# One layer of a hybrid streaming encoder: three MLP banks, one ring of four for scores and transposes, and a block's row factors in one bank

## The chip, the cores and the metric

The kernel is one program on one core of a Trainium2 chip. The metric is the device time of one execution in microseconds (us). Its time before is the median of three runs. One more execution was recorded by the hardware profiler, and all rows shown here are from that execution.

The names of the engines are those of the profile: PE is TensorE's matrix multiplication and PEld its loading of weights, DVE is VectorE, ACT is ScalarE, POOL is GpSimd, SP is SyncE, whose queue (SPq) starts nearly all DMA transfers of this kernel.

## What is computed

One layer of an encoder over a prompt of 2048 tokens and a sample of 32, at a width of 1024. Cut to what matters:

```python
a = rmsnorm(h, g_attn)                 # per token: h * r * g, r = rsqrt(mean(h*h) + eps)
qa, ka, va, qb, kb, vb = split(a @ w_in)
# group A, long range: 4 heads, two q/k maps of 64 dims per head, 128-dim values
s = einsum('bqhmd,bkhmd->bhmqk', qa, ka) * 64 ** -0.5 + t5_bias
p = softmax(where(key_chunk <= query_chunk, s, NEG))
oa = (p[:, :, 0] - lam * p[:, :, 1]) @ va
# group B, band: 8 heads of 64, a chunk of 64 sees itself and the 8 chunks before it
ob = softmax(qb @ kb.T * 64 ** -0.5 + clip_bias) @ vb
h = h + concat(rmsnorm(oa) * (1 - lam_init), rmsnorm(ob)) @ w_out
h = h + square(relu(rmsnorm(h, g_mlp) @ w_up)) @ w_down          # width 4096
h = h + sigmoid(h @ w_ple_gate) * (p_emb @ w_ple_proj)
y = rmsnorm(h, g_final)
```

The keys and values of the prompt and the sample are outputs too; the sample also attends to 128 cached positions. All is float32.

## The kernel before

**Numbers.** A float32 product is made of three matmuls on rounded halves: each operand is split into a high part and the rest (`split`), and `mm3` (lines 212 to 218) accumulates high x high, high x rest and rest x high into one PSUM tile. So a weight piece of 512 KB is loaded by SP (`wr`), its high part (`wh` or `piece`) is written by ACT at line 181, and the rest (`wl`) by POOL or DVE.

**Blocks.** The tokens are cut into four blocks of 512; the last has the 32 sample tokens too. Activations stand transposed, features on partitions.

**Stages.** `prep` loads a block's tokens in tiles of 128, transposes them (`xp`), splits them (`aH`, `aL`) and makes each token's factor r: ACT squares and sums the row, `rsqrt` makes r in ACT and DVE steps (`rsv`, `rsy`), and it lands in a column of `rcol`, one token a partition. To scale products whose tokens lie along a row, the column is spread and transposed into a PSUM tile `rp` (line 393), and ACT copies it to the block's row tile `rbt` (line 394). `proj` makes q, k and v; its evictions of q and k (`qps`, lines 477 and 482) multiply by that row. `attn_a` is the long-range part: JA0 does the query pairs 0 to 3 (256 queries each), JA1 the pairs 4 and 5 and then 6, 7 and the sample (index 8), each for four heads. `attn_b` is the band part. `outproj`, `mlp` (`ups` is an up product, `dps` a down product), `gate` (`gps`, `pps`) and `final` (`yp`) follow by block.

**A pair in the long-range part** (`attn_a_pair`, lines 597 to 729). For each of two query tiles and two maps: score matmuls into a PSUM tile `s` of 512 keys (line 639), eviction by DVE into `e` with the running maximum (lines 646 and 648), exponential on ACT (654), the two maps joined on DVE (660). Then for each four key tiles: transposes of `e` into a PSUM tile `tpp` (698), its halves `pH` by ACT (705) and `pL` by DVE (706), and the products with v into `o` (712 to 714). A sum of squares (`ss`) and a normalisation end the pair. The keys of a head come in tiles of 1024 (`ka`, three buffers), the queries in `q` (two buffers).

**PSUM.** All pools together have eight banks, tiles of 128 x 512 float32. `mm` has two, and a third, `mmx`, joins it in a ring until the second half of the band part is done; then it is given to the long-range scores as `psy`. Scores have `ps_s` (two), transposes `ps_t` (two), outputs `ps_o` (one). A tile of a ring waits until its bank's last user has been read. When attention is over, six banks are opened again as `md`.

**Order.** The program is written as one sequence, but a scheduler with a model of the engines' times orders each engine's instructions before the run. So the output projections and MLPs of blocks 0 and 1, which need nothing of JA1, are spread by it among the scores of JA1 on PE. On the chip each engine and the SP queue go strictly in that order: an instruction that waits holds up all behind it.

## Time and profile before

| | |
|---|---|
| median of three runs | 3122.03 us (3116.57 to 3123.8) |
| the profiled execution | 3116.1 us |
| its span, first to last instruction | 3114.0 us |
| instructions | 51781 |
| long-range scores of JA1 on PE | 1229.88 to 1888.3 us |
| last output matmul of JA1 on PE | 1928.8 us |
| gate of block 1 on PE | from 2029.2 us |

How to read the rows that follow: a row of stages or windows has its stretch in us, its width, and the busy time of PE, PEld, DVE, ACT and POOL with their counts, then the granted clock of TensorE (1 is full), the busy share of the DMA engines and GB/s. A row of waits has the waiting engine, tile and line, what ended the wait, then total us, times, and the longest. A row of the timeline has start, duration, engine, line, operation, output and inputs, and in brackets the idle time of that engine just before, with what ended it. A row of a tile has shortest, median and longest duration in ns, and first and last start.

### The profile page before, as it was taken

To read this page: it belongs to the slowest core of one execution; us is meant where nothing else is said; L and a number is where in the kernel's file an instruction comes from. 1 tells how busy PE (TensorE), PEld (TensorE's weight loads), DVE (VectorE), ACT (ScalarE), POOL (GpSimd) and SP (SyncE) were. 2 spreads that over 40 slices of the span, in tenths; PEclk is the share of its full clock that TensorE was granted. 3 is DMA by queue.
4 is the path that set the end of the run, shared out by engine and by line. 5 is a ranking of instruction groups with operands and counts; after the bars stand their busy time and mean duration, and the time that the engine had idled before them with its cause. 6 is when DMAs were issued, how large, how long until landed. Compare 5 with 4: busy or idle time off the path is not lost. (4 is left out here: it accounts for less than half of the span.)

```text
span 3114.0 us, 51781 instructions
## 1 busy us (share of the span) xinstructions
PE 2992.9 (96%) x17801; PEld 2639.7 (85%) x17801; DVE 1815.1 (58%) x4404; ACT 1779.4 (57%) x3446; POOL 1859.1 (60%) x2512
## 2 busy tenths in 40 slices
PE   8998988999999999999999999999899999999998
PEld 7787877999877887788788888779788887999998
DVE  5256574654466554566655654425667884576663
ACT  6256665765666774566655645454655545554545
POOL 2456745423445543665645556677878888767674
PEclk9999999999999999999999999999999999999999
DMA  9797866976788555565665443538434446333231
GB/s 285 261 263 226 243 199 211 269 225 197 213 248 268 154 148 139 151 172 147 192 173 146 126 122 108 162 98 261 154 116 136 139 159 223 117 109 102 89 117 57
DMA packets 523278, 539.19 MB, mean 173 GB/s; under 512 B 38748, under 2 KB 401568, under 8 KB 523016
## 3 DMA queue, kind: packets, MB, share of 16 engines
q1 hardware_dynamic: 523016, 535.89, 57.3%
q8 instruction: 141, 2.31, 0.3%
q14 instruction: 121, 0.99, 0.1%
HBM read 421.97 MB, written 117.75 MB: 173 GB/s over the span
## 5 line engine op out<-in xcount | busy, mean ns | idle before, releaser
L176 POOL TENSOR_TENSOR wl<-wr,wh 128x256 fp32r<-128x256 f32 x648 | 482.3, 776 | 322.6 <-ACT wh L181 271.2
L181 ACT ACTIVATE piece<-wr 128x512 fp32r<-128x512 f32 x406 | 245.8, 625 | 269.2 <-PE ups L217 116.0
L176 POOL TENSOR_TENSOR piece<-wr,piece 128x256 fp32r<-128x256 f32 x404 | 326.5, 834 | 101.9 <-ACT piece L181 80.7
L181 ACT ACTIVATE wh<-wr 128x1024 fp32r<-128x1024 f32 x228 | 240.5, 1056 | 224.7 <-PE ups L217 56.8
L166 POOL TENSOR_TENSOR wl<-wr,wh 128x256 fp32r<-128x256 f32 x264 | 197.2, 777 | 166.9 <-ACT wh L181 162.0
L216 PE MATMUL dps<-uh,piece 128*128 128x272 f32 (+1 forms) x768 | 246.4, 324 | 7.2 <-ACT piece L181 2.9
L166 POOL TENSOR_TENSOR piece<-wr,piece 128x256 fp32r<-128x256 f32 x280 | 234.4, 868 | 27.8 <-ACT piece L181 24.9
L1158 DVE TENSOR_TENSOR h<-h,dps 128x512 f32<-128x512 f32 x256 | 174.2, 683 | 130.1 <-PE dps L218 128.6
L218 PE MATMUL dps<-uh,piece 128*128 128x272 f32 (+1 forms) x768 | 247.1, 324 | 1.3 <-POOL piece L166 1.1
L217 PE MATMUL dps<-ul,piece 128*128 128x272 f32 (+1 forms) x768 | 247.3, 323 | 0.2 <-DVE ul L187 0.2
L216 PE MATMUL ups<-cs,piece 128*128 128x256 f32 (+1 forms) x864 | 245.7, 285 | 1.6 <-DVE r L1217 1.6
L217 PE MATMUL ups<-cs,piece 128*128 128x256 f32 (+1 forms) x864 | 245.7, 285 | 0.0
L218 PE MATMUL ups<-cs,piece 128*128 128x256 f32 (+1 forms) x864 | 245.5, 284 | 0.0
L216 PE MATMUL qps<-aH,wh 128*128 128x512 f32 (+1 forms) x640 | 228.6, 357 | 1.2 <-DVE ql L477 0.9
L217 PE MATMUL qps<-aL,wh 128*128 128x512 f32 (+1 forms) x640 | 227.2, 355 | 0.0
L218 PE MATMUL qps<-aH,wl 128*128 128x512 f32 (+1 forms) x640 | 227.0, 355 | 0.0
L1206 DVE TENSOR_TENSOR h<-h,dps 128x272 f32<-128x272 f32 (+1 forms) x384 | 189.1, 514 | 51.9 <-PE dps L218 51.1
L216 PE MATMUL dps<-uh,wh 128*128 128x512 f32 x512 | 211.6, 413 | 7.0 <-ACT relu L1123 4.4
L654 ACT ACTIVATE e<-e,nm 128x128 f32<-128x128 f32 (+16 forms) x136 | 157.1, 1156 | 97.4 <-DVE nm L652 96.9
L217 PE MATMUL dps<-ul,wh 128*128 128x512 f32 x512 | 203.5, 397 | 0.0
L218 PE MATMUL dps<-uh,wl 128*128 128x512 f32 x512 | 203.1, 397 | 0.0
L216 PE MATMUL ups<-cH,wh 128*128 128x512 f32 x512 | 202.0, 395 | 0.5 <-ACT relu L1123 0.5
(310 smaller groups left out, 9370.5 us busy)
## 6 DMA issues: line engine op xcount, KB each, us to landing
wr<-w_up SPq DMA_DIRECT2D x128, 512.0 KB, 3.9
wr<-w_down SPq DMA_DIRECT2D x128, 512.0 KB, 3.8
wr<-w_in SPq DMA_DIRECT2D x74, 512.0 KB, 5.5
q<-qS SPq DMA_DIRECT2D x128, 256.0 KB, 5.6
v<-vSa SPq DMA_DIRECT2D x64, 512.0 KB, 3.6
ka<-kS SPq DMA_DIRECT2D x32, 512.0 KB, 8.0
wr<-w_out SPq DMA_DIRECT2D x32, 512.0 KB, 5.0
wr<-w_ple_gate SPq DMA_DIRECT2D x32, 512.0 KB, 4.2
```

The source lines that it names most:

```text
L166: nc.gpsimd.tensor_tensor(out[:, sl], a[:, sl], b[:, sl], op=op)
L176: nc.gpsimd.tensor_tensor(out[:, sl], a[:, sl], b[:, sl], op=op)
L181: nc.scalar.activation(hi, raw, AF.Copy)
L216: nc.tensor.matmul(ps, lh, rh, start=start and i == 0, stop=False)
L217: nc.tensor.matmul(ps, lh, rl, start=False, stop=False)
L218: nc.tensor.matmul(ps, ll, rh, start=False, stop=stop and i == n - 1)
L654: nc.scalar.activation(row, row, AF.Exp, bias=nmx, accum_out=z[:nr, m : m + 1])
L1158: nc.vector.tensor_tensor(hv, hv, ps, op=ALU.add)
L1206: nc.vector.tensor_tensor(hv, hv, ps, op=ALU.add)
```

## The change

There are two edits.

In `prep` the transposes of the row factors are kept in a list while the block's tiles are made. After the fourth tile one PSUM tile `rp` is taken, the four transposes write its four quarters, and one copy of 512 columns goes to `rbt`. Block 3 takes another tile for the sample's 32 tokens.

In `run` the ring of `mm` and `mmx` keeps its three banks through the output projections, norms and MLPs of blocks 0 and 1, and the gate of block 1. The long-range part JA1 takes scores and transposes alike from one ring of four, `ps_s`, `ps_t`, `ps_s`, `ps_t` in turn. The gate of block 1 stands ahead of the closing of the attention pools, in the ring of three, where it had the six banks of `md`.

```diff
@@ prep
         aH, aL = acts[b]
+        late = []
         for i, (c0, n) in enumerate(toks(b)):
...
             self.rsqrt(pp, st[:n], 1, 1.0 / D, EPS, nc.vector, "r1", n, out=r)
+
+            def spread(r=r, c0=c0, n=n):
+                nc.tensor.transpose(rp[:, c0 % 512 : c0 % 512 + n], r.broadcast_to([n, P]), self.ident[:n, :n])
+
+            late.append(spread)
+            yield
+        rp = mm.tile([P, 512], F32, tag=tag, name="rp")
+        for f in late[:4]:
+            f()
+        nc.scalar.activation(self.rb[b][:, :512], rp, AF.Copy)
+        if b == 3:
             rp = mm.tile([P, 512], F32, tag=tag, name="rp")
-            nc.tensor.transpose(rp[:, :n], r.broadcast_to([n, P]), self.ident[:n, :n])
-            nc.scalar.activation(self.rb[b][:, c0 : c0 + n], rp[:, :n], AF.Copy)
-            yield
+            late[4]()
+            nc.scalar.activation(self.rb[b][:, 512 : 512 + SS], rp[:, :SS], AF.Copy)
@@ run
-            mz = mm
+            mm0 = mz = mm
             mm = Rings((mz, "mm"), (mz, "mm"), (opened(mmx, "mmx", 1, PSUM), "mm"))
...
-            mmx.close()
-            mm = mz
-            ps_y = opened(psx, "psy", 1, PSUM, "right")
-            sy = Rings((ps_s, "s"), (ps_s, "s"), (ps_y, "s"))
+            mz = mm
+            sy = Rings((ps_s, "s"), (ps_t, "tp"), (ps_s, "s"), (ps_t, "tp"))
...
-                    self.attn_a(js, pool, sy, ps_t, ps_o)
+                    self.attn_a(js, pool, sy, sy, ps_o)
...
+            drain(self.gate(1, h, uq, actq, mm))
             psx.close()
+            mmx.close()
+            mm = mm0
             md = opened(top, "md", 8 - MM, PSUM, "right")
-            drain(self.gate(1, h, uq, actq, md))
             drain(self.final(1, h, uq, fk, mm))
```

Since the scheduler orders all anew, instructions move far beyond these lines. Three places follow, the second on two engines, each before and then changed; the line numbers in the changed rows are up to 2 higher inside `prep` and 11 higher between it and `run`. (On PE from the middle of `final(1)` on, about 2140 us, the two orders are the same.)

PE at the second token tile of block 2, where a row factor is transposed (`rp`), among products for v and the long-range part JA0. Before:

```order
L713 MATMUL o_2532<-pL_2536,v_2533 128x128
L714 MATMUL o_2532<-pH_2535,v_2533 128x128
L379 MATMUL xp_4656<-ident_113,x_4637 128x128 x4
L393 MATMUL rp_4680<-ident_113,rcol_124 128x128
L698 MATMUL tpp_2778<-ident_113,e_2683 128x128
L216 MATMUL vps_4701<-wh_4685,aH_107 128x256
L217 MATMUL vps_4701<-wl_4686,aH_107 128x256
L218 MATMUL vps_4701<-wh_4685,aL_108 128x256
```

Changed, the place where block 2's four factors are transposed, among the matmuls of its first q product:

```order
L217 MATMUL qps_5032<-aL_108,wh_5022 128x512
L218 MATMUL qps_5032<-aH_107,wl_5023 128x512
L216 MATMUL qps_5032<-aH_107,wh_5022 128x512
L395 MATMUL rp_5105<-ident_113,rcol_124 128x128 x4
L650 MATMUL s_2974<-ka_2952,q_2955 128x384 x2
L650 MATMUL s_2978<-ka_2952,q_2955 128x256 x2
L217 MATMUL qps_5032<-aL_108,wh_5022 128x512
L218 MATMUL qps_5032<-aH_107,wl_5023 128x512
```

The transpose stood directly behind the tile's own token transposes and ahead of an attention transpose; now four stand together, after the fourth tile, between a q product and scores.

The SP queue where the last head of the long-range part starts: `ka_16305` and `ka_16277` are its second key tile, `q_16313` and `q_16285` the queries of its pair 6, `q_16544` those of pair 7. Before:

```order
L157 DMA v_16121<-vSa_86 128x4x256
L157 DMA wr_21799<-w_up 128x8x128
L157 DMA ka_16305<-kS_85 64x2x1024 x2
L157 DMA q_16313<-qS_84 64x2x512
L157 DMA ks_16306<-kS_85 64x2x160 x2
L157 DMA q_16313<-qS_84 64x2x512
L157 DMA q_16544<-qS_84 64x2x512 x2
L157 DMA wr_21841<-w_down 128x2x512
```

Changed:

```order
L157 DMA wr_22518<-w_down 128x2x512
L157 DMA wr_22559<-w_up 128x8x128
L157 DMA ka_16277<-kS_85 64x2x1024 x2
L157 DMA q_16285<-qS_84 64x2x512 x2
L157 DMA wr_22601<-w_up 128x8x128
L157 DMA wr_22643<-w_down 128x2x512
L157 DMA v_16123<-vSa_86 128x4x256
L157 DMA oT_88<-os_15942 128x256
```

The sample's keys (`ks`) and the next pair's queries, which stood between and right behind these queries, now come later, and weights stand there.

PE at the same head's start, from the last score on the head before (`ka_15752`, `ka_15724`) to the first on its own keys (`ka_16304`, `ka_16276`). Before, with 20 further rows of down products left out:

```order
L639 MATMUL s_16078<-ka_15752,q_15991 128x512 x2
L639 MATMUL s_16243<-ks_15753,q_16232 32x160 x2
L639 MATMUL s_16249<-ks_15753,q_16232 32x160 x2
L216 MATMUL dps_21692<-uh_21434,wh_21677 128x512
L217 MATMUL dps_21692<-ul_21435,wh_21677 128x512
L218 MATMUL dps_21692<-uh_21434,wl_21678 128x512
...
L639 MATMUL s_16322<-ka_16304,q_16313 128x512 x2
L639 MATMUL s_16330<-ka_16305,q_16313 128x384 x2
```

Changed, with up and down products, transposes and outputs left out:

```order
L650 MATMUL s_16050<-ka_15724,q_15963 128x512 x2
L216 MATMUL ups_22446<-cH_20378,wh_22437 128x512
L217 MATMUL ups_22446<-cL_20379,wh_22437 128x512
L218 MATMUL ups_22446<-cH_20378,wl_22438 128x512
...
L650 MATMUL s_16215<-ks_15725,q_16204 32x160 x2
...
L725 MATMUL o_16062<-pH_16126,v_16123 128x256
L650 MATMUL s_16221<-ks_15725,q_16204 32x160 x2
L650 MATMUL s_16294<-ka_16276,q_16285 128x512 x2
L216 MATMUL ups_22570<-cH_20378,wh_22561 128x512
```

From 28 matmuls the distance went to 143.

ACT in the gate of block 1, where `sig` is the sigmoid's tile, `wh` a weight piece, and `ou` the split attention rows of block 2 (from `oraw`, loaded for it). Before:

```order
L181 ACTIVATE wh_23415<-wr_23413 128x1024
L1351 ACTIVATE sig_23347<-gps_23322 128x512
L1352 ACTIVATE sig_23347<-sig_23347 128x512
L1353 ACTIVATE sig_23347<-sig_23347 128x512
L1356 ACTIVATE sig_23347<-sig_23347 128x512
L181 ACTIVATE wh_23424<-wr_23422 128x1024
L1351 ACTIVATE sig_23397<-gps_23372 128x512
L181 ACTIVATE wh_23474<-wr_23472 128x1024
```

Changed:

```order
L1362 ACTIVATE sig_23312<-gps_23287 128x512
L1363 ACTIVATE sig_23312<-sig_23312 128x512
L1364 ACTIVATE sig_23312<-sig_23312 128x512
L181 ACTIVATE ou_20426<-oraw_20442 128x512
L181 ACTIVATE ou_20427<-oraw_20446 128x512
L1367 ACTIVATE sig_23312<-sig_23312 128x512
L181 ACTIVATE ou_20428<-oraw_20450 128x512
L181 ACTIVATE ou_20429<-oraw_20454 128x512
L181 ACTIVATE wh_23389<-wr_23387 128x1024
```

The splits of block 2's attention rows stood among the MLP of block 1 before, and now stand inside the chain from a gate product to its sigmoid.

## The prediction

> **What bounds the kernel now.** I read the page's first part, then the span by stages, then what TensorE (PE) waited for, then its timeline at the longest waits.

> ```profile
> PE 2992.9 (96%) x17801; PEld 2639.7 (85%) x17801; DVE 1815.1 (58%) x4404; ACT 1779.4 (57%) x3446; POOL 1859.1 (60%) x2512
> core 0: 3114.0 us, clock 0.986
> ```

> TensorE is busy 96% of the span and no other engine passes 60%. So 3114.0 - 2992.9 = 121.1 us of TensorE idleness, and the stretches in which its granted clock is below 1, are all that a new order can win; the work itself is 17801 matmuls in both kernels. From the stages on which this rests (columns: width, then busy time of PE, PEld, DVE, ACT, POOL, then clock, DMA share, GB/s):

> ```profile
> 1215.00:1300.00 85.00, 76.46 (x358) 63.12 (x358) 41.70 (x102) 45.10 (x69) 44.93 (x62) 0.95 0.71 181
> 1300.00:1590.00 290.00, 285.93 (x1488) 241.61 (x1488) 195.47 (x461) 180.84 (x279) 178.33 (x239) 1.00 0.58 169
> 1590.00:1930.00 340.00, 332.31 (x1732) 281.11 (x1731) 193.82 (x467) 192.27 (x300) 186.44 (x264) 0.99 0.46 130
> 1930.00:2140.00 210.00, 207.12 (x910) 167.66 (x909) 89.78 (x130) 97.31 (x165) 149.99 (x207) 0.99 0.49 154
> 2140.00:3114.00 974.00, 939.25 (x6439) 876.48 (x6438) 628.22 (x1095) 512.38 (x991) 718.69 (x876) 0.99 0.41 132
> ```

> The long-range part of the change is 1215 to 1930: there TensorE idles 8.5 + 4.1 + 7.7 = 20.3 us, and the clock takes 0.05 x 76.5 + 0.01 x 332.3 = 7.1 us more. 27 us is thus the most that part can give. From 2140 on TensorE's order is the same row for row, so that stage's 34.8 us stay. What ended the waits (total, count, longest):

> ```profile
> PE s L639 <- DMA q<-qS: 10.9, 5, 3.8
> PE sb L820 <- DVE stb L823: 7.7, 4, 2.9
> PE s L639 <- DVE e L646: 4.6, 4, 1.4
> PE ops L216 <- ACT oact L181: 4.5, 1, 4.5
> PE dps L216 <- ACT relu L1123: 4.4, 2, 4.0
> ```

> Score and transpose banks are hardly in it: 4.6 us of scores on their eviction in the whole span. What costs is rare and long, and three of these waits stand at the start of a head:

> ```profile
> 1229.88 1.99 PE L639 MATMUL s<-ka,q 128*128 128x512 f32 x8 [2.44 <-DMA q<-qS]
> 1235.55 1.37 PE L639 MATMUL s<-ka,q 128*128 128x512 f32 x8
> 1258.10 1.09 PE L698 MATMUL tpp<-ident,e 128*128 128x128 f32 x8 [2.01 <-DVE e L660]
> 1296.57 0.80 PE L216 MATMUL dps<-uh,wh 128*128 128x512 f32 x1 [4.01 <-ACT relu L1123]
> 1690.24 1.17 PE L639 MATMUL s<-ka,q 128*128 128x512 f32 x4 [2.71 <-DMA q<-qS]
> 1793.48 1.58 PE L639 MATMUL s<-ka,q 128*128 128x512 f32 x4 [3.81 <-DMA q<-qS]
> ```

> The eight score matmuls after the wait at 1229.88 took 1.99 us, the next eight 1.37: after such a wait the clock is halved for a while. In windows of 8 us:

> ```profile
> 292.00:300.00 8.00, 7.44 (x36) 7.00 (x37) 6.31 (x19) 3.10 (x8) 4.22 (x7) 0.58 0.73 233
> 1228.00:1236.00 8.00, 6.12 (x22) 5.22 (x23) 2.87 (x10) 1.35 (x2) 0.00 (x0) 0.79 1.08 269
> 1296.00:1304.00 8.00, 7.43 (x29) 6.27 (x30) 2.79 (x5) 4.83 (x10) 7.89 (x12) 0.61 0.57 191
> 1688.00:1696.00 8.00, 5.76 (x20) 4.60 (x21) 4.07 (x6) 2.40 (x3) 3.60 (x4) 0.79 1.07 230
> 1792.00:1800.00 8.00, 6.52 (x26) 5.52 (x27) 2.85 (x4) 0.67 (x2) 2.03 (x2) 0.79 0.60 171
> ```

> [...]

> **The change part by part.** Everything is summed against the profiled execution's own 3116.1 us (span 3114.0); the median shown, 3122.0, lies 5.9 above it.

> *Row factors (T1).* Seventeen transposes stay seventeen; ScalarE's copies go from 17 to 5, at no gain, as ScalarE is not the bound. What goes is the place: a transpose no longer stands directly behind its own factor's chain on DVE.

> ```profile
> 40.09 0.32 PE L393 MATMUL rp<-ident,rcol 128*128 128x128 f32 x1 [2.65 <-DVE rsv L229]
> 292.27 1.27 DVE L706 TENSOR_TENSOR pL<-tpp,pH 128x512 fp32r<-128x512 f32 x2
> 292.50 0.45 PE L393 MATMUL rp<-ident,rcol 128*128 128x128 f32 x1 [4.41 <-DVE rcol L231]
> 293.00 0.18 PEld L698 LDWEIGHTS tpp<-ident,e 128*128 128x128 f32 x1 [0.36 <-DVE pL L706]
> ```

> High end: 2.65 + 4.41 us of waits, and 0.42 x 7.44 = 3.1 us of halved clock after the second, 10.2. Low end 0: the attention transpose behind it waited for DVE's pL, which began at 292.27, hence until 293.00 anyway if DVE keeps that order. I take 4, nearer the low end, because of that row. The factors in row form now come late, after all four tiles; the new order puts the four transposes within a block's first q product, whose eviction needs them, and ScalarE's one 512-wide copy takes 0.6 us, as the pH row below has for this size; two further mm banks cover it. Price 0, and 0.6 us a block if they are full. In the first two blocks the four are spread over the block's tiles, so one of that ring's four banks is held meanwhile; at worst that brings the 2.65 back.

> *Head starts (T2).* Between the last score on one head's keys and the first on the next one's, the last three heads had 36, 23 and 28 matmuls on TensorE; the new order has 157, 143 and 143, of which 72 or more are 512 wide. Between the last band product and the first long-range score stood 52 wide ones, now 77. The second key tile's load can only start when that last score has read its buffer:

> ```profile
> 1781.83 1.23 SPq L157 DMA_DIRECT2D ka<-kS  x2
> 1783.86 0.57 SPq L157 DMA_DIRECT2D q<-qS  x1
> 1234.18 0.39 PE L216 MATMUL dps<-uh,wh 128*128 128x512 f32 x1
> 1234.41 0.39 PE L217 MATMUL dps<-ul,wh 128*128 128x512 f32 x1
> ```

> At this head the loads began at 1781.83 and the score ran at 1793.48: 11.65 us. Wide matmuls start 0.23 us apart (1234.18, 1234.41), so 72 cover 16.6 us, and at the first head 25 more cover 5.8, against a wait of 2.44. The three waits are 2.44 + 2.71 + 3.81 = 9.0 us and their clock 0.21 x (6.12 + 5.76 + 6.52) = 3.9. High end 12.9, low end 0 (the queue is as full as before and something else waits for it). I take 11, since both covers exceed what is waited for.

> *Weights behind a head's loads (T3).* At 1296.57 a down product waited 4.01 us; the clock added 0.39 x 7.43 = 2.9. On the queue stood:

> ```profile
> 1279.96 1.23 SPq L157 DMA_DIRECT2D ka<-kS  x2
> 1283.14 1.26 SPq L157 DMA_DIRECT2D ka<-kS  x2
> 1284.51 8.49 SPq L157 DMA_DIRECT2D wr<-w_up  x2
> ```

> ScalarE was held by a weight piece behind four key loads. The new order issues the same bytes, so this can go (+6.9) or come twice (-6.9). I take +3: the second pair of key loads is no longer needed at once.

> *One ring of four (T4).* A bank's next user may now be the other kind. Holding times:

> ```profile
> L646 DVE TENSOR_SCALAR_CACHE_REDUCE e<-s x160: 541/685/694, 1230.6 to 1885.8; 128x512 f32<-128x512 f32 x144, 128x384 f32<-128x384 f32 x16
> L705 ACT ACTIVATE pH<-tpp x120: 178/592/611, 1253.1 to 1921.7; 128x512 fp32r<-128x512 f32 x88, 128x128 fp32r<-128x128 f32 x8, 128x256 fp32r<-128x256 f32 x8, 128x384 fp32r<-128x384 f32 x8
> L706 DVE TENSOR_TENSOR pL<-tpp,pH x120: 169/681/693, 1253.7 to 1921.9; 128x512 fp32r<-128x512 f32 x88, 128x128 fp32r<-128x128 f32 x8, 128x256 fp32r<-128x256 f32 x8, 128x384 fp32r<-128x384 f32 x8
> ```

> A score bank is held 0.69 us after its last matmul and a transpose bank 0.59 + 0.68 = 1.27, plus queueing. Behind a waiting score, the products of the other blocks on TensorE wait too. All score waits on evictions in the old span are 4.6 us, and the softmax wait at 1258.10 is 2.0. Bounds: all of it goes, +6.6, or the first rival below. I take -2, because two kinds now share what each had alone.

> *Gate of block 1 in three banks (T5).*

> ```profile
> L1351 ACT ACTIVATE sig<-gps x8: 578/582/597, 2043.2 to 2086.1; 128x512 f32<-128x512 f32 x8
> L1355 DVE SCALAR_TENSOR_TENSOR sig<-gps,sig x8: 692/692/693, 2045.2 to 2089.4; 128x512 f32<-128x512 f32 x8
> ```

> A gate bank is held from 2043.2 to 2045.9, 2.7 us, and the next gate and projection groups are 30 matmuls, 30 x 0.23 = 6.9 us: hidden, with 4 us to spare. But ScalarE now splits the attention rows of block 2 between the sigmoid's steps and waits for their loads there; a wait of that kind cost 4.5 us above (ops on oact). Bounds 0 and three of those, -13.5; I take -2.

> *Third bank, rest of the order (T6).* Before 1215 the third MLP bank lets more products stand among the band-attention scores (850 up and down matmuls between the first and the last of them, 563 before), whose waits are 7.7 us. Bounds +7.7 and -7.7, I take +3.

> Sum: 4 + 11 + 3 - 2 - 2 + 3 = 17; 3116.1 - 17 = 3099, and 5.9 more for the median: **3105 us**.

> **The rivals.** *Slower: scores and transposes lock each other.* In one ring the next pair's scores cannot run past the last transposes, so the softmax chain, which at 1258.10 already let TensorE wait 2.01 us, shows at each pair. There are 4 x 4 pairs and 4 sample tiles; if half wait as long, and each halves the clock for as much again as the waits above (3.9 on 9.0), that is 10 x 2.01 x 1.43 = 29, T4 becomes -29: 3105 + 27 = 3132. It decides from about seven such waits on: 7 x 2.87 = 20, more than the rest of the sum wins. For it: between a query tile's last score and its first transpose stand 51.5 matmuls in the middle of 36 tiles, 55 before. Against it: a bank's next user stands at least 11 matmuls behind its last, 10 before. [...]

> *No change: the queue is the bound at a head's start.* DMA share is above 1 in two of the windows (1.08, 1.07). If the loads merely meet the weights, T2 and T3 are 0 and the rest gives 3: 3119.

> *Late end.* The old order has 394 up and down matmuls of block 1 behind the last attention matmul, the new one none: attention ends inside the gate. If the rows of block 2 come late, T5 is -13.5 and 3105 + 11.5 = 3117, about no change or slower.

> *More than forecast.* All of 27 in the long-range part and 10 by T1: 3122 - 37 = 3085.

> **How the numbers follow.** What a measurement can tell is 0.2%, 6.2 us: faster is below 3115.8, slower above 3128.3. Chances: forecast 45%, more than forecast 15%, no change 14%, late end 10%, slower 16%. Faster: the first two, 0.60; same: most of no change and a third of late end, 0.16; slower: the last and the rest, 0.24. Range 3084 to 3134: the lower end is the fourth rival, the upper the first; the forecast alone would be 3092 to 3115.

> **What would show it.** Right: no score wait on q above 1 us at the starts of the last three heads, clock 1.00 there, 1215 to the end of attention with under 12 us idle; no rp group among the waits. Wrong: many short waits of s or tpp on DVE, a wait of gps on sig, ops on ou or oact before 2140, or another start time of the unchanged last stage than 17 us earlier.

## The result, and the profile after

| kernel | median of its runs, us | lowest to highest, us | ratio of the changed kernel to the one before |
|---|---|---|---|
| before | 3122.91 (4 runs) | 3116.57 to 3123.96 | |
| changed | 3103.43 (4 runs) | 3100.72 to 3106.68 | 0.9937, 95% interval 0.9918 to 0.9955 |
| changed, timed once more later | 3101.35 (6 runs) | 3095.60 to 3105.94 | 0.9938, 0.9925 to 0.9952 |

The change makes the kernel 0.63% faster, 19.5 us; 3105 us was forecast. The profiled execution of the changed kernel took 3106.68 us, its slowest of the four, while that of the kernel before was its fastest. A pair of first profiles therefore shows less than the medians do, 3114.0 - 3104.9 = 9.1 us of span.

The page's first part and its span, for the changed kernel:

```profile
PE 2990.2 (96%) x17801; PEld 2637.0 (85%) x17801; DVE 1826.0 (59%) x4404; ACT 1776.4 (57%) x3434; POOL 1852.7 (60%) x2512
core 0: 3104.9 us, clock 0.988
```

The work is the same, 17801 matmuls; ScalarE has 12 instructions fewer, the row copies. What changed is idle time and clock. The span by the same stretches as before (width, then busy time of PE, PEld, DVE, ACT, POOL, then clock, DMA share, GB/s):

```profile
1215.00:1300.00 85.00, 85.00 (x412) 69.93 (x411) 42.43 (x123) 52.35 (x102) 47.65 (x69) 1.00 0.41 125
1300.00:1590.00 290.00, 280.93 (x1431) 236.14 (x1430) 178.84 (x420) 164.94 (x259) 173.20 (x233) 0.99 0.60 172
1590.00:1930.00 340.00, 337.29 (x1764) 286.07 (x1763) 210.41 (x504) 200.44 (x305) 188.98 (x273) 1.00 0.52 144
1930.00:2140.00 210.00, 202.84 (x1003) 168.68 (x1002) 114.09 (x202) 112.40 (x201) 139.81 (x190) 0.99 0.50 156
```

From 1215 to 1930 TensorE idles 0 + 9.1 + 2.7 = 11.8 us, where it idled 20.3, and the clock's shortfall, 7.1 us before, is 0.01 x 280.9 = 2.8 us. The stretch 1930 to 2140, where attention now ends, went the other way: 7.2 us idle, 2.9 before. The waits of TensorE in the whole span show both (total, count, longest):

```profile
PE sb L831 <- DVE stb L834: 13.8, 13, 3.4
PE s L650 <- DVE e L657: 6.8, 4, 4.9
PE css L1096 <- ACT sh L181: 5.9, 1, 5.9
PE gps L216 <- DVE sig L1381: 3.1, 1, 3.1
PE ops L216 <- ACT oact L181: 1.9, 1, 1.9
PE s L650 <- DMA q<-qS: 0.4, 1, 0.4
```

The wait of scores for q, 10.9 us before, is 0.4. The row factors (rp) no longer stand among the waits, which held 7.7 us of them before. Three things are new: band scores wait 13.8 us for their eviction where it was 7.7, a column sum (css) waits 5.9 us once, and a gate product waits 3.1 us for the sigmoid.

The stages of the two kernels end at other times, since the filler moved. So I cut every kernel at the same events: 520 us, the last band product, the last softmax sum (ss) of attention, and the first gate product of the tail whose order is unchanged (gps from hu). In each stage the **loss** is TensorE's idle time plus (1 - clock) x busy time, added up over windows of 20 us:

| kernel | to 520 | band part | long-range part | gate to tail | unchanged tail | sum |
|---|---|---|---|---|---|---|
| before | 43.4 | 35.0 | 27.9 | 5.7 | 40.6 | 152.6 |
| before, second profile | 42.3 | 34.3 | 29.0 | 5.0 | 39.5 | 150.1 |
| changed | 40.6 | 39.7 | 14.1 | 11.1 | 37.3 | 142.8 |
| changed, second profile | 35.9 | 35.6 | 14.6 | 8.7 | 42.8 | 137.6 |

Span less sum is 2961.4, 2963.8, 2962.1 and 2961.0 us: the same work within 3 us, so the table accounts for the times. The changed kernel gains 14 us in the long-range part and 2 to 8 us before 520 us, and gives back 3 to 6 between attention's end and the tail and up to 5 in the band part. A stage of a single execution is certain to some 5 us only, as the two rows of the changed kernel show.

### The profile page after: what moved, and what is told of

It is laid out like the page before. It is cut to its first block, busy times and chain, and to the rows that moved or that the text cites. A ratio compares the mean times of both kernels' runs of the same rounds, so it can differ in the third digit from the quotient of the medians.

```text
span 3104.9 us, 51763 instructions
## 1 busy us (share of the span) xinstructions
PE 2990.2 (96%) x17801; PEld 2637.0 (85%) x17801; DVE 1826.0 (59%) x4404; ACT 1776.4 (57%) x3434; POOL 1852.7 (60%) x2512
## 5 line engine op out<-in xcount | busy, mean ns | idle before, releaser
L181 ACT ACTIVATE piece<-wr 128x512 fp32r<-128x512 f32 x406 | 245.4, 624 | 265.0 <-PE ups L217 111.2
L181 ACT ACTIVATE wh<-wr 128x1024 fp32r<-128x1024 f32 x228 | 240.4, 1055 | 188.1 <-PE ups L217 46.8
L216 PE MATMUL dps<-uh,piece 128*128 128x272 f32 (+1 forms) x768 | 246.3, 324 | 6.2 <-DVE h L1217 2.5
L217 PE MATMUL dps<-ul,piece 128*128 128x272 f32 (+1 forms) x768 | 247.3, 323 | 0.2 <-DVE ul L187 0.2
L216 PE MATMUL ups<-cs,piece 128*128 128x256 f32 (+1 forms) x864 | 245.8, 285 | 0.9 <-DVE r L1228 0.8
L217 PE MATMUL ups<-cs,piece 128*128 128x256 f32 (+1 forms) x864 | 245.7, 285 | 0.0
L216 PE MATMUL qps<-aH,wh 128*128 128x512 f32 (+1 forms) x640 | 227.9, 357 | 1.1 <-DVE ql L488 1.1
L217 PE MATMUL qps<-aL,wh 128*128 128x512 f32 (+1 forms) x640 | 228.0, 356 | 0.0
L216 PE MATMUL dps<-uh,wh 128*128 128x512 f32 x512 | 207.0, 404 | 1.8 <-DVE h L1169 1.8
L216 PE MATMUL ups<-cH,wh 128*128 128x512 f32 x512 | 202.8, 397 | 1.9 <-ACT cH L181 1.9
L217 PE MATMUL ups<-cL,wh 128*128 128x512 f32 x512 | 202.5, 396 | 1.8 <-POOL cL L166 1.2
L218 PE MATMUL ups<-cH,wl 128*128 128x512 f32 x512 | 202.7, 396 | 0.0
```

Source lines behind the costliest of these rows:

```text
L181: nc.scalar.activation(hi, raw, AF.Copy)
L216: nc.tensor.matmul(ps, lh, rh, start=start and i == 0, stop=False)
L217: nc.tensor.matmul(ps, lh, rl, start=False, stop=False)
L218: nc.tensor.matmul(ps, ll, rh, start=False, stop=stop and i == n - 1)
```

## The experiments

Each kernel was timed in five rounds beside the kernel before on the same chip. Losses are given in the order of the table above.

**The row factors alone.** The new `prep`, with the old banks.

```diff
         r = self.rcol[:n, 4 * b + i : 4 * b + i + 1]
...
+            late.append(spread)
+            yield
+        rp = mm.tile([P, 512], F32, tag=tag, name="rp")
+        for f in late[:4]:
+            f()
...
```

> The row-factor edit alone on the kernel before (two MLP banks, the old rings). Theory, by the first term of the sum: the waits of rp on DVE (7.6 us in all before) are gone, of which about 4 us is kept: 3119 us against 3123 before; q waits of scores at the starts of heads stay at about 10 us in all. Rival (any new order moves the time, whatever its cause): a time anywhere from 3108 to 3135, with rp waits gone all the same. Second rival (the whole gain is in this edit): 3103.

Measured: 3120.68 us (11 runs), ratio 1.0007, 0.9999 to 1.0016. The time lies within 2 us of the 3119 expected, but the kernel before took 3119.35 us beside it: where a gain of some 4 us was expected, there is none. Losses: 38.7 to 520 us (43 before), 40.9 in the band part (35), 32.4 in the long-range part (28), 5.3 and 39.5. The waits of rp are gone and some 4 us with them, and both later stages give it back. The wait of band scores for their eviction says where in the band part, first the kernel before, then this one:

```profile
PE sb L820 <- DVE stb L823: 7.7, 4, 2.9
```

```profile
PE sb L831 <- DVE stb L834: 20.2, 15, 4.3
```

Band scores now wait 20.2 us for a score bank, against 7.7; their waits for q fell from 6.2 to 2.6 us. The longest of these waits, on the timeline of all engines:

```profile
992.29 0.69 DVE L187 TENSOR_TENSOR sl<-sqacc,sh 128x512 fp32r<-128x512 f32 x1 [1.37 <-ACT sh L181]
...
996.42 1.41 DVE L998 SCALAR_TENSOR_TENSOR tmp<-tmp,g_mlp_s,rl 128x512 f32<-128x512 f32 x2 [3.16 <-DMA tmp<-hS]
...
997.75 0.48 DVE L834 CUSTOM_DVE_ANT_0 eb<-sb,bb 128x320 f32<-128x320 f32 x1
...
998.30 0.85 PE L831 MATMUL sb<-kbt,q 128*128 128x320 f32 x2 [4.33 <-DVE stb L834]
```

VectorE took these rows one after the other. Its next row was the norm of block 0's rows (tmp), which waited 3.16 us for a load, and the eviction of the score bank, behind it in the order, started at 997.75 us; TensorE waited 4.33 us for that eviction. In this place the order has a row that waits for DMA ahead of an eviction. But such meetings are not new. The three longest of these waits in the kernel before (2.4, 2.9 and 1.5 us) stand behind VectorE rows that had waited for DMA as well, here the second:

```profile
937.40 0.75 DVE L940 SCALAR_TENSOR_TENSOR oraw<-oraw,g_b_s,rb 128x512 f32<-128x512 f32 x1 [2.78 <-DMA oraw<-oT]
...
938.61 0.98 PE L820 MATMUL sb<-kbt,q 128*128 128x320 f32 x4 [2.90 <-DVE stb L823]
```

And of the six waits above 1.2 us in this run, 14.7 us together, two (4.3 and 3.1 us) stand behind a VectorE row that waited for DMA, the others behind rows that waited for ScalarE or GpSimd. So the row shown is an example; that the new `prep` brings more such waits is measured, by what way is not shown.

**The banks alone.** The new `run`, with the old `prep`.

```diff
-            mmx.close()
-            mm = mz
...
-                    self.attn_a(js, pool, sy, ps_t, ps_o)
+                    self.attn_a(js, pool, sy, sy, ps_o)
...
+            drain(self.gate(1, h, uq, actq, mm))
             psx.close()
+            mmx.close()
```

> The banks edit alone (three MLP banks, one ring of four, gate in three banks), with the old row factors, one transpose and one copy a tile. Theory: the head starts keep their cover, score waits on q under 1 us in all, rp waits return (about 7 us), 3107 us. Rival (any new order moves the time): 3095 to 3125 with no relation to the q waits. Second rival (the gain is all in the row factors): 3120.

Measured: 3111.92 us (12 runs), ratio 0.9977, 0.9967 to 0.9987: half the gain forecast. Losses 42.9, 40.1, 12.6, 14.1, 41.6. The long-range part is won in full (12.6 against 28), 5 us are lost in the band part and 9 in the gate. The waits of rp are back (4.5 us). The q waits are 4.1 us in all, where under 1 was expected; the longest, 2.4 us, stands at the first long-range head. Band scores wait for their eviction 6.4 us, no more than before.

So the long waits of band scores come with the new `prep`, not with the third bank.

**The third bank without the common ring.** Scores take their two banks and transposes theirs.

```diff
-                    self.attn_a(js, pool, sy, sy, ps_o)
+                    self.attn_a(js, pool, ps_s, ps_t, ps_o)
```

> The changed kernel, but JA1's scores in their own two banks and its transposes in their own two, instead of one ring of four. Theory: the third MLP bank spreads the attention and so covers the head starts (q waits under 2 us), but two score banks make scores wait for DVE, 3 to 8 us more than in the changed kernel: 3108 us. Rival (the ring is what frees the order, the third MLP bank is idle cover): 3118. Second rival (the ring does nothing): 3103.

Measured: 3172.35 us (4 runs), ratio 1.0165, 1.0151 to 1.0178, far outside the expectation. The long-range loss is 66.1 us. Its windows, and the long waits in them:

```profile
1286.50:1590.00 303.50, 292.23 (x1424) 241.71 (x1422) 169.83 (x372) 163.34 (x250) 182.46 (x248) 0.99 0.59 168
1590.00:1930.00 340.00, 340.00 (x1718) 287.46 (x1717) 179.44 (x410) 185.17 (x269) 201.51 (x282) 1.00 0.48 135
1930.00:2136.90 206.90, 166.53 (x833) 133.37 (x831) 124.61 (x321) 116.50 (x209) 77.07 (x115) 0.90 0.35 104
```

```profile
PE tpp L709 <- DVE e L671: 16.0, 6, 5.1
PE s L650 <- DVE e L657: 6.9, 13, 1.2
```

From 1590 to 1930 us TensorE does not idle at all: the filler with three banks goes ahead and attention with two score banks lags. Then the filler is used up (the last down product starts at 1950 us, the last gate product of block 1 at 2020), attention runs on alone to 2137 us, and in the last 207 us TensorE idles 40 at a clock of 0.90, the largest share, 14.7 us, in transposes that wait for the softmax's last step (e). Here the third bank for the filler had to be paid with banks for attention.

**The common ring without the third bank.** The multilayer part keeps two banks, and the gate its six.

```diff
+            mmx.close()
+            mm = mm0
             sy = Rings((ps_s, "s"), (ps_t, "tp"), (ps_s, "s"), (ps_t, "tp"))
...
             psx.close()
             md = opened(top, "md", 8 - MM, PSUM, "right")
+            drain(self.gate(1, h, uq, actq, md))
```

> The changed kernel, but with the MLP, output projection and norms of blocks 0 and 1 in two banks from JA1 on as before, block 1's gate in the six banks; one PSUM bank stays unused during JA1, and JA1 keeps the ring of four. Theory: without the third bank attention runs ahead as before and the products between a head's last score and the next head's first are few again: q waits of 6 to 10 us, 3114 us. Rival (the ring alone spreads the attention): q waits under 2 us, 3104.

Measured: 3117.77 us (11 runs), ratio 0.9988, 0.9979 to 0.9996. Neither expectation holds whole. The q waits fall to 2.5 us and the long-range loss to 20.6, so the ring alone does spread attention over the head starts, as the rival said; but the band part (44.1, with 19.0 us of band scores on their eviction) and the tail of that execution (44.8) take it back, and the time lies beyond the theory's 3114. What stands in the long-range part instead is the filler's own wait, down products for the eviction of the one before (into h):

```profile
PE dps L216 <- DVE h L1169: 9.2, 8, 5.4
```

In the changed kernel, with the third bank, that wait is 1.8 us in this stage.

**The gate behind attention again.** The changed kernel, with the gate of block 1 in six banks.

```diff
-            drain(self.gate(1, h, uq, actq, mm))
             psx.close()
             mmx.close()
             mm = mm0
             md = opened(top, "md", 8 - MM, PSUM, "right")
+            drain(self.gate(1, h, uq, actq, md))
```

> The changed kernel with one thing undone: the gate of the last block's first half stands behind the closing of the score and product pools again, and so has six banks instead of three. The orders at the starts of the heads are those of the changed kernel. Theory (the gate in three banks took back about 5 us, T5): the loss of the stage from the last softmax wait to the first product of the unchanged tail falls from 11 us to about 6, no wait of a gate product on the sigmoid, 3098 to 3100 us, 1.3 times 0.1% under the changed kernel's 3103. Rival (what was lost there comes from attention now ending late, not from the gate's banks): loss still 10 to 14 us and 3103 or more; if the gate can only begin when the last score bank is free, 3106.

Measured: 3110.88 us (12 runs), ratio 0.9967, 0.9956 to 0.9979, 7 to 10 us slower than the changed kernel. The theory fell: the loss from the softmax sum to the tail is 10.6, as in the changed kernel, and the long-range part loses 27.5 us, where the changed kernel loses 14. The place is attention's last softmax sum, here on the timeline of several engines (the profiled execution took 3118.94 us, the slowest of the twelve, so its losses may lie at the high end):

```profile
2016.88 0.39 PE L218 MATMUL dps<-uh,wl 128*128 128x512 f32 x1
...
2021.83 2.08 POOL L176 TENSOR_TENSOR wl<-wr,wh 128x256 fp32r<-128x256 f32 x3
2023.87 0.72 POOL L231 TENSOR_TENSOR rsy<-rsy,rsv 128x256 f32<-128x256 f32 x1
...
2025.43 0.37 PE L734 MATMUL ss<-sh,ones_r 128*128 128x32 f32 x1 [7.46 <-DVE sh L183]
```

The last rows of attention need a reciprocal root on GpSimd, and its steps stand between weight pieces (wl) that GpSimd splits. The multilayer part has ended, the gate cannot begin, and TensorE waits 7.46 us. The clock falls with it, in windows of 8 us:

```profile
2016.00:2024.00 8.00, 1.97 (x9) 1.33 (x9) 2.56 (x4) 2.31 (x4) 8.00 (x12) 0.93 0.22 66
2024.00:2032.00 8.00, 6.57 (x21) 5.40 (x22) 0.90 (x3) 1.00 (x4) 2.11 (x8) 0.64 0.52 159
```

In the changed kernel gate products stand there. Taken as a whole, the gate in three banks is no loss: it covers attention's end, and by the medians it is worth 7 to 10 us.

**The changed kernel again.** No edit.

> The changed kernel itself once more, beside the others on one chip. Expected: 3103 us, ratio 0.994; the losses by stage within 2 us of those of its first profile (40.6, 39.7, 14.1, 11.1, 37.3), apart from the unchanged tail, whose length differs by some 5 us from execution to execution.

Measured: 3101.35 us (6 runs), ratio 0.9938, 0.9925 to 0.9952. The time repeats. The losses are 35.9, 35.6, 14.6, 8.7 and 42.8: the first two stages are 4 to 5 us below the first profile, more than the 2 us expected. The long-range part repeats within 0.5 us.

**A neutral reorder of the kernel before.** One number in the weaving of the position preparation.

```diff
-                weave(qk, self.prep_p(sg, wk, ps_t), 2)
+                weave(qk, self.prep_p(sg, wk, ps_t), 3)
```

> The kernel before with one neutral change: the preparation of the position products is woven into the q and k products of the first part at every third step instead of every second; no bank, buffer or head start is touched. Theory (the gain comes from the head starts in the long-range part): within 0.2% of the kernel before, 3114 to 3126, with the waits on q at the head starts unchanged in kind (some 8 to 11 us). Rival (any other order of so tightly packed a program moves the time by as much): outside 0.2%, and the waits on q gone or moved with no bank changed.

Measured: 3114.45 us (11 runs), ratio 0.9983, 0.9973 to 0.9993. Within 0.2%, as the theory has it, but not nothing: an order that touches none of the changed things gains 0.17%. Losses 37.5, 45.1, 23.7, 4.8, 41.1; the q waits are 5.8 us, fewer than the 8 to 11 expected. What a chance order gave here is thus about a quarter of the change's gain. The 14 us of the long-range part are more than that: with the old banks that stage lost 27.9, 29.0, 32.4 and 23.7 us, with three banks, the common ring and the gate inside 14.1, 14.6 and 12.6, and 16.8 and 9.8 in two kernels further below.

**Two banks for block 0.** The changed kernel, with the third bank only from block 1 on.

```diff
-                m = self.mlp((b,), {b: (h,) + cn[b]}, wk, uq, mm, mm)
+                mb = mm if b else mm0
+                m = self.mlp((b,), {b: (h,) + cn[b]}, wk, uq, mb, mb)
```

The output products of blocks 0 and 1 and their norms get `mm0` in the same way.

> The changed kernel, but the output products of the first two blocks and the multilayer part of block 0 use two of the three banks; only block 1 and its gate use all three. Theory (the third bank costs about 5 us in the band stage and is needed only beside the long-range heads): the loss of the stage from 520 us to the end of band attention falls from 39.7 to about 35, the long-range stage stays at 13 to 16, 3099 us. Rival (without the third bank in block 0 the filler falls out of step with attention, as with the ring alone): long-range loss 20 or more, 3110 to 3116.

Measured: 3113.51 us (8 runs), ratio 0.9977, 0.9965 to 0.9989. The theory fell and the rival holds. The long-range loss is 24.3 us, and the band part, which was to fall to 35, rises to 46.1, with 18.8 us of band scores on their eviction in it.

With the new `prep`, band scores wait 18.8 to 20.2 us where two banks serve the filler (three kernels) and 12.0 to 14.8 where three do (the changed kernel twice, and four others). The third bank is a gain in the band part, once the row factors are moved.

**The column sum one step later.** The changed kernel, aimed at its 5.9 us wait.

```diff
-            if n in (at[0] + i * at[1], at[0] + i * at[1] + at[2]):
+            if n in (((8, 9), (9, 11))[i] if at is ONQ else (at[0] + i * at[1], at[0] + i * at[1] + at[2])):
```

The wait in the changed kernel, first the DMA queue, then ScalarE and TensorE:

```profile
1289.17 1.52 SPq L157 DMA_DIRECT2D oraw<-oT  x3
...
1295.70 2.59 SPq L157 DMA_DIRECT2D ka<-kS  x4
1298.33 1.26 SPq L157 DMA_DIRECT2D q<-qS  x2
...
1305.08 1.74 SPq L157 DMA_DIRECT2D ka<-kS  x2
...
1312.34 0.34 SPq L157 DMA_DIRECT2D oraw<-oT  x1
```

```profile
1320.48 0.66 ACT L932 ACTIVATE oraw<-oraw 128x544 f32<-128x544 f32 x1 [7.34 <-DMA oraw<-oT]
...
1324.11 0.64 ACT L181 ACTIVATE sh<-sqacc 128x544 fp32r<-128x544 f32 x1
```

```profile
1324.80 0.82 PE L1096 MATMUL css<-sh,ones_r 128*128 128x272 f32 x2 [5.93 <-ACT sh L181]
...
1325.87 0.63 PE L217 MATMUL dps<-ul,wh 128*128 128x512 f32 x1
1326.30 0.63 PE L218 MATMUL dps<-uh,wl 128*128 128x512 f32 x1
```

Three of the four rows to be summed were loaded at 1289; the fourth stands on the queue behind all of a head's keys and queries and starts at 1312.34, so the sum comes late. From 1323 to 1329 us the clock is halved, 0.50 in each window of 1 us: products that start 0.23 us apart elsewhere (2030.81 and 2031.04 us) start 0.43 us apart.

> The changed kernel with the column sum of the last block's attention rows (css of block 3) one step of block 0's multilayer part later. In the changed kernel that product waited 5.9 us at the first long-range head, because the fourth of the four rows it sums is loaded behind that head's key and query loads. Theory (that wait and the halved clock behind it are a cost of the new order that can be taken off): no css wait above 1 us, the long-range loss falls from 14 us to about 6, 3095 us. Rival (the wait is only a meeting point of heads and filler; with it gone the next thing waits, or the changed order behind it loses as much): long-range loss 12 or more, 3100 to 3105.

Measured: 3101.74 us (6 runs), ratio 0.9933, 0.9920 to 0.9946: the changed kernel's own time. The wait is gone, as the theory had it, and the rival holds all the same. The long-range loss is 16.8 us, for two other waits stand in the same stage. The first comes from the same late load:

```profile
1312.30 0.66 ACT L932 ACTIVATE oraw<-oraw 128x544 f32<-128x544 f32 x1 [7.70 <-DMA oraw<-oT]
```

```profile
1317.08 0.80 PE L216 MATMUL dps<-uh,wh 128*128 128x512 f32 x1 [3.96 <-ACT relu L1134]
```

The edit moved the product, not the load. ScalarE still waited 7.70 us for the fourth row, and the eviction (relu) that a down product needed stood behind that row. The second is a score that waits for a transpose's eviction, once:

```profile
PE s L650 <- DVE pL L717: 3.6, 1, 3.6
```

**The kernel before again.** No edit.

> The kernel before itself, once more with a profile, to see how far its losses by stage differ from one execution to another. Expected: 3119 to 3123 us, ratio 1.000; the q waits at the same three heads, the long-range loss within 4 us of 27.9, the other stages within 5 us of 43.4, 35.0, 5.7 and 40.6. Rival (the long-range loss of the first profile was an accident of that execution): below 22 us or above 34.

Measured: 3120.83 us (12 runs), ratio 0.9997, 0.9986 to 1.0008. The q waits are 10.3 us, and each stage's loss is within 1.2 us of the first profile: the 28 us of the long-range part were no accident. Its profiled execution took 3116.0 us, again the lowest of its runs.

**Later column sum and the other weaving together.**

> The later column sum together with the weaving of the position preparation at every third step, which alone made the kernel before 0.17% faster. If the two add to the change: 3090 us. Rival (the 0.17% belonged to that one order and does not carry over to another): the same as the kernel with the later column sum alone, or slower by up to 0.2%.

Measured: 3108.23 us (6 runs), ratio 0.9947, 0.9927 to 0.9966. The 0.17% of the other weaving doesn't carry over; the rival holds, beyond its 0.2% by the medians alone, though the intervals of the two ratios overlap. The long-range loss is the smallest of all, 9.8 us, and the band part's 43.0 takes it back. No kernel here beats the changed one by more than can be told.

## Why the prediction was right, and where its steps were not

The forecast of 3105 us and the side were right; that the time came within 2 us of it is in part luck. The stages' sum is 11.1 us won, 6 less than forecast. Against that stands the 5.9 us added for the median: it was the distance of one execution of the kernel before, and the changed kernel's profiled executions lay 3.2 us above and 1.0 us below their medians. The two misses nearly cancel. The terms, against the mean losses of two profiles of each kernel:

| term | forecast, us won | measured |
|---|---|---|
| T1 row factors, to 520 us | +4 | +4.6 |
| T6 third bank in the band part | +3 | -3.0 |
| T2, T3, T4 long-range part | +11 + 3 - 2 = +12 | +14.1 |
| T5 gate | -2 | -4.6 |
| unchanged tail | 0 | 0.0 |
| sum | 17 | 11.1 |

**T1 held, in its own stage.** The three profiles with the old `prep` and the old weaving lose 42.9 us on average up to 520 us, the eight with the new `prep` and that weaving 39.0. Two limits: the other weaving, with the old `prep`, lost 37.5 us there, so a chance order can give that stage as much; and other waits came up in the changed kernel, such as one of a score for its eviction, 4.9 us (6.0 in the second profile), where the longest was 1.4. What the step left out is the order behind it: band scores wait longer for their eviction, and where two banks serve the filler the later stages gave all of the gain back.

**T2 held.** The q waits in the long-range part fall from 9.7 us to 0.4 (1.2 in the second profile), and that stage's clock shortfall from 7.6 to 2.3 us. The cover was the step's reason, and the traces bear it out. Between the last score on one head's keys and the first on the next, at the last three heads, the four profiles with the old rings have 22 to 36 matmuls on TensorE, and 11 of these 12 starts wait 0.7 to 4.1 us for q. The eight profiles with the ring of four have 120 to 179, and none of 24 starts waits for q. The ring alone, with two banks for the filler, has 120, 169 and 126 there, so the ring and not the third bank makes the cover; the third bank with rings apart has 40, 47 and 13, and waits 3.2 us at the last. What the step overrated is the cover at the first head: there a q wait stays in all eight, 0.4 and 1.2 us in the changed kernel and up to 3.6 us in the others.

**T3 had the wrong sign, as far as the list of waits tells.** T2, T3 and T4 were measured only together. The wait of a down product on ScalarE, 4.4 us in this stage, is gone from the list. But a load behind a head's loads is late as before: now it is the fourth row of the column sum, 5.9 us and the clock. The run that moved the waiting product won nothing, because the load stayed late and held ScalarE in its place. I had summed such waits as if each stood alone.

**T4 had the wrong sign, by the same list.** I took -2 for more waits of scores and transposes; in the long-range part the longest wait of a score is now 0.8 us and none of a transpose is listed, where 1.4 and 2.0 us stood before. The two lists of that stage, the kernel before first:

```profile
PE s L639 <- DMA q<-qS: 9.7, 4, 3.8
PE dps L216 <- ACT relu L1123: 4.4, 2, 4.0
PE tpp L698 <- DVE e L660: 2.0, 1, 2.0
PE s L639 <- DVE e L646: 1.4, 1, 1.4
```

```profile
PE css L1096 <- ACT sh L181: 5.9, 1, 5.9
PE o L723 <- DMA v<-vSa: 2.3, 2, 1.9
PE dps L216 <- DVE h L1169: 1.8, 4, 0.8
PE s L650 <- DVE mx L659: 0.8, 1, 0.8
```

The slower rival, scores and transposes locking each other, shows in no row of the changed kernel, and once, 3.6 us, in the run with the later column sum. The softmax waits that it feared come with the rings apart, 16.0 us of transposes in the run with the third bank alone. The danger was two score banks, not one ring of four: the ring, which this step priced as a cost, is what makes the cover of T2.

**T5 was undersized.** The loss behind attention rose by 4.6 us. What the step feared came once in each profile of the changed kernel, a gate product waiting 3.1 and 2.1 us for the sigmoid, though the wait ends on VectorE and not on ScalarE. VectorE's rows of that chain in the first profile:

```profile
2048.17 1.90 DVE L951 SCALAR_TENSOR_TENSOR oraw<-oraw,g_b_s,rb 128x512 f32<-128x512 f32 x2 [4.28 <-DMA oraw<-oT]
2050.00 0.68 DVE L1366 SCALAR_TENSOR_TENSOR sig<-gps,sig 128x512 f32<-128x512 f32 x1
...
2054.80 0.67 DVE L1381 TENSOR_TENSOR sig<-sig,pps 128x512 f32<-128x512 f32 x1
```

Between the last two rows stand four rows of block 2's attention, in both profiles, and the last row is what the gate product waited for. The gate bank, which the step had as held for 2.7 us, was held from 2044.05 to 2050.68 us, 6.6 us: ScalarE's third step came 3.1 us late, behind a weight piece that waited 2.16 us for its load, and VectorE's next row stood behind the rows of block 2 (oraw) that had waited 4.28 us for theirs. With six banks, behind attention, no gate product waits for the sigmoid, but others wait up to 2.6 us, and that stage loses as much (10.6 us) and 13 us more is lost in the stage ahead of it, over half of it at attention's last sum. So six banks were no remedy: with them attention's late end, the third rival, cost more.

**T6 had the wrong sign in the sum, for two causes that I had in one.** Band scores wait longer because of the new `prep` (7.7 to 20.2 us with two banks), and the third bank takes some 6 us of that back. Without the new `prep` the third bank cost 5 us in that part, in one profile.

So the parts do not add: the row factors alone give 1.0007, the banks alone 0.9977, both 0.9937. What shows of it is one direction: the third bank takes back part of what the new `prep` costs in the band part. By stage, in these few profiles, the changed kernel loses less than its two parts would add up to by some 9 us in the band part, 4 in the gate and 2 in the long-range part.

Of the signs named: no q wait above 1 us at the last three heads (true in both profiles; the 1.2 us of the second stands at the first head), clock 1.00 there, 11.8 us idle (12.1 in the second) where under 12 was named, no rp among the waits. Of the signs of error two came: a gate product waiting for the sigmoid, 3.1 and 2.1 us, and the start of the unchanged tail, which was to be 17 us earlier and was 6.9 us earlier in the first pair of profiles (2189.1 and 2182.2), 17.4 in the second (2188.9 and 2171.5). A wait of ops on oact, named too, stands in the band part as before, 1.9 us where it was 4.5.

**What stays open.** The profiles show 12.2 us of span between the means of both kernels, the medians 19.5. Both profiled executions of the kernel before were the lowest of their series; where its other executions lose their 5 us more, no profile here shows. Why band scores wait longer with the new `prep` is open too: no run moved the VectorE rows that stand ahead of the evictions. Nor is it known why the banks alone lose 5 us in the band part, where band scores wait no longer than before.

## What to carry to other kernels

Where attention and a filler shared the matrix engine here, banks decided how fast each advanced: a third bank for the filler was worth something only where attention's banks were shared in one ring (3103.43 us, and 3172.35 with the rings apart), and more where a third job with banks of its own was ready for attention's end (3110.88 us with the gate behind attention). Cut the span at events, not at times, and compare losses stage by stage with a second profile of each kernel before believing a difference of 5 us. A wait in the list is not a gain to be had: moving the product that waited 5.9 us gained nothing, because the late load behind it then held another engine for 7.70 us, while an order that put more work between the heads gained 14 us in its stage. Follow a wait back to what was late, and change that.

## What the runs showed of the hardware

```profile
2055.53 0.50 PE L216 MATMUL gps<-hH,wh 128*128 128x512 f32 x1 [3.14 <-DVE sig L1381]
```

```profile
2056.00:2064.00 8.00, 8.00 (x30) 6.41 (x29) 2.51 (x4) 2.10 (x4) 4.76 (x7) 0.79 1.08 324
2057.00:2058.00 1.00, 1.00 (x3) 0.79 (x3) 0.82 (x2) 0.14 (x1) 1.00 (x2) 0.50 0.99 285
```
